# Two MLPs whose second product runs partly with seven block products: the order of the pairs in a job, the half of the features that is summed, and when weights are asked for

## The chip, the cores and the metric

One core of a Trainium2 chip runs the whole program. The metric is the time of the program on the device in microseconds (us), the median of several runs. Engines by the names of the profile: PE is TensorE (PEld its weight loads), DVE is VectorE, ACT is ScalarE, POOL is GpSimd, SP is SyncE. PSUM has eight banks here, which the kernel calls mm (four), sb (two) and tb (two).

## What is computed

A decoder trunk of two layers on 256 tokens of 2048 features in float32. Each layer has an attention part, which the change does not touch, and an MLP:

```python
def sq_relu_mlp(h, w1, w2):
    return jnp.square(jax.nn.relu(h @ w1)) @ w2      # w1 2048 x 8192, w2 8192 x 2048
...
f = sq_relu_mlp(rms_norm(h, g_ffn_pre), *ffns[layer])
h = h + rms_norm(f, g_ffn_post)
```

## The kernel before

Every float32 operand is cut in two (`split`: a rounded high part by ACT, L246 or with the norm's gain L249; the rest by DVE, L247 or L250), and a product is three matmuls: high by high, high by low, low by high.

An MLP runs over four blocks of 2048 of the 8192 features. In a block **ff1** makes the block's features from `uT` and `w1`, in two jobs of 1024 features (`job_T`): eight units of 128 features, each in a PSUM bank of its own, over 16 k of 128 rows, two k at a time; a k of a unit is a matmul of 512 columns (L409) and one of 256 (L413). (The first half of block 0 is done by other jobs.) When a unit is complete, ACT copies (L402) and DVE adds (L403) its halves; of two units ACT then does relu and square (L733, L734) and the split into `hT`: a pair of 128-feature tiles, eight pairs in a block. Pairs 0 to 3 come from ff1's first job, 4 to 7 from its second.

**ff2** multiplies the block by its rows of `w2`, in two jobs of 1024 output columns, c = 0 and c = 1 (`job_7`). Each job goes over the eight pairs. A *plain* pair is 2x2 blocks times 2x2 blocks with 8 products. A *seven* is the same with 7 products of sums of blocks, into eight banks c11, c12, c21, c22 (as in a plain pair) and p1, p5, p6, p7, which are put together later. A seven needs sums of features (`Sevens.put`: DVE L485 to L489, then a split, `sums`) and sums of weights (DVE L525 to L527, `wsum`, whose split is `wboth`). Each product is three matmuls of 512 columns (L564). The order is 0, 4, 1, 5, 2, 6, 3, 7, with 4 to 7 sevens. So a job has 4 x 8 + 4 x 7 = 60 products, 180 matmuls, and it ends on a seven. In block 3 only c = 0 is done so; c = 1 is a plain job.

In blocks 0 to 2 each of the eight banks that a job ends with is copied by ACT to one of six tiles `s` (L767) and added by a DMA of POOL into `acc` in DRAM, 256 KB each (plain writes in block 0, L769; accumulating ones from block 1 on, L771). In block 3 `combine` (L783) reads them all back by SP's queue while ff1's first job runs, and DVE adds them up (L796).

The c banks are mm; p1 and p6 are sb; p5 and p7 are tb. The units of an ff1 job take mm x4, sb x2, tb x2 (`all_banks`). Weights come by SP's queue into three 1 MB tiles `raw`; each job's own generator asks for a `raw` and its split just ahead of the matmuls that use them in the written order. A scheduler then sets the order of each engine; the time of a wait is read from the trace only.

## Time and profile before

| | us |
|---|---|
| median of 3 runs | 2341.24 (2337.76 to 2345.25) |
| the profiled execution | 2339.55 |
| its span, first to last instruction | 2337.8 |
| PE busy | 2256.1 (97%) |
| DVE, ACT, POOL busy | 1624.5, 1405.9, 128.7 |
| mean granted clock of PE | 0.983 |

The span is one execution; the 1.75 us between it and the execution's time lie around it. A busy share is an average over all stages, so a stage has to be read by itself: its length against the matmuls in it, and what PE waits for there. The granted clock is 1.00 at 2.4 GHz and 0.50 at 1.2 GHz.

### The profile page before, as it was taken

To read this page: it belongs to the slowest core of one execution; us is meant where nothing else is said; L and a number is where in the kernel's file an instruction comes from. 1 tells how busy PE (TensorE), PEld (TensorE's weight loads), DVE (VectorE), ACT (ScalarE), POOL (GpSimd) and SP (SyncE) were. 2 spreads that over 40 slices of the span, in tenths; PEclk is the share of its full clock that TensorE was granted. 3 is DMA by queue.
4 is the path that set the end of the run, shared out by engine and by line. 5 is a ranking of instruction groups with operands and counts; after the bars stand their busy time and mean duration, and the time that the engine had idled before them with its cause. 6 is when DMAs were issued, how large, how long until landed. Compare 5 with 4: busy or idle time off the path is not lost. (4 is left out here: it accounts for less than half of the span.)

```text
span 2337.8 us, 31006 instructions
## 1 busy us (share of the span) xinstructions
PE 2256.1 (97%) x11781; PEld 1921.1 (82%) x11781; DVE 1624.5 (69%) x2483; ACT 1405.9 (60%) x2180; POOL 128.7 (6%) x144
## 2 busy tenths in 40 slices
PE   9999999999999999999999999999999999989997
PEld 8889888788788877877888888887788877877876
DVE  5877557695685687597565677847695685587586
ACT  5766557565565665576556666657565665564664
POOL 0000010000011011001000000011000011011002
PEclk9999999999999999999999999999999999999999
DMA  7744346466477479554554554555476477559653
GB/s 243 240 145 149 132 164 216 159 237 232 158 241 232 162 214 293 198 221 179 192 194 148 182 167 159 178 180 198 144 249 239 160 233 219 196 167 294 223 204 138
DMA packets 148722, 460.60 MB, mean 197 GB/s; under 512 B 9046, under 2 KB 9820, under 8 KB 147036
## 3 DMA queue, kind: packets, MB, share of 16 engines
q1 hardware_dynamic: 136220, 429.25, 53.5%
q0 software_dynamic: 12352, 29.37, 5.7%
q8 instruction: 92, 1.51, 0.3%
q14 instruction: 58, 0.48, 0.1%
HBM read 427.12 MB, written 31.46 MB: 196 GB/s over the span
## 5 line engine op out<-in xcount | busy, mean ns | idle before, releaser
L250 DVE SCALAR_TENSOR_TENSOR wlo<-raw,gT,whi 128x512 fp32r<-128x512 f32 (+4 forms) x621 | 606.6, 1009 | 404.3 <-PE tb L413 168.5
L249 ACT ACTIVATE whi<-raw,gT 128x512 fp32r<-128x512 f32 (+4 forms) x621 | 551.4, 928 | 401.1 <-PE tb L409 187.7
L409 PE MATMUL mm<-uT,whi 128*128 128x512 f32 x1952 | 504.4, 394 | 1.2 <-ACT whi L249 0.9
L247 DVE TENSOR_TENSOR wlo<-raw,whi 128x1024 fp32r<-128x1024 f32 x304 | 374.3, 1245 | 139.1 <-ACT whi L246 134.2
L246 ACT ACTIVATE whi<-raw 128x1024 fp32r<-128x1024 f32 x304 | 313.2, 1055 | 147.7 <-PE mm L365 66.7
L409 PEld LDWEIGHTS mm<-uT,whi 128*128 128x128 f32 x1952 | 347.3, 189 | 59.9 <-ACT whi L249 1.4
L564 PE MATMUL mm<-whi,hT 128*128 128x512 f32 x1120 | 359.9, 393 | 0.0
L413 PEld LDWEIGHTS mm<-uT,wlo 128*128 128x128 f32 x1952 | 273.9, 192 | 25.0 <-DVE wlo L250 2.3
L413 PE MATMUL mm<-uT,wlo 128*128 128x256 f32 x1952 | 283.3, 284 | 2.0 <-DVE wlo L250 2.0
L564 PEld LDWEIGHTS mm<-whi,hT 128*128 128x128 f32 x1120 | 212.9, 190 | 44.7
L564 PE MATMUL mm<-wlo,hT 128*128 128x512 f32 x560 | 219.5, 392 | 0.6 <-DVE wlo L247 0.6
L365 PE MATMUL mm<-whi,uT 128*128 128x512 f32 (+1 forms) x640 | 197.0, 398 | 0.0
L564 PE MATMUL tb<-wboth,sums 128*128 128x512 f32 x336 | 100.9, 425 | 35.0 <-ACT wboth L246 35.0
L365 PEld LDWEIGHTS mm<-whi,uT 128*128 128x128 f32 x640 | 115.9, 189 | 19.7
L409 PE MATMUL tb<-uT,whi 128*128 128x512 f32 x448 | 125.3, 395 | 5.8 <-ACT s L767 5.8
L409 PE MATMUL sb<-uT,whi 128*128 128x512 f32 x448 | 123.5, 391 | 4.4 <-ACT s L767 4.4
L564 PEld LDWEIGHTS mm<-wlo,hT 128*128 128x128 f32 x560 | 105.6, 189 | 25.2 <-DVE wlo L247 3.6
L564 PEld LDWEIGHTS tb<-wboth,sums 128*128 128x128 f32 x336 | 66.9, 204 | 54.0 <-ACT wboth L246 38.4
L246 ACT ACTIVATE wboth<-wsum 128x1024 fp32r<-128x1024 f32 x56 | 59.5, 1062 | 85.8 <-DVE wsum L525 84.0
L365 PE MATMUL mm<-wlo,uT 128*128 128x512 f32 x320 | 104.8, 385 | 1.1 <-DVE wlo L250 1.1
L409 PEld LDWEIGHTS tb<-uT,whi 128*128 128x128 f32 x448 | 81.4, 189 | 23.6 <-ACT s L767 7.6
L409 PEld LDWEIGHTS sb<-uT,whi 128*128 128x128 f32 x448 | 81.8, 188 | 21.1 <-ACT s L767 6.1
(305 smaller groups left out, 3186.2 us busy)
## 6 DMA issues: line engine op xcount, KB each, us to landing
raw<-in_l_w_ff_dram SPq DMA_DIRECT2D x256, 1024.0 KB, 5.0
raw<-in_l_w_in_dram SPq DMA_DIRECT2D x87, 1024.0 KB, 5.1
raw<-in_l_w_out_dram SPq DMA_DIRECT2D x24, 1024.0 KB, 4.8
raw<-in_l_w_in_dram SPq DMA_DIRECT2D x8, 832.0 KB, 4.6
acc0c<-s POOLq DMA_DIRECT2D x24, 256.0 KB, 7.4
acc0p<-s POOLq DMA_DIRECT2D x24, 256.0 KB, 10.9
acc1c<-s POOLq DMA_DIRECT2D x24, 256.0 KB, 7.2
acc1p<-s POOLq DMA_DIRECT2D x24, 256.0 KB, 10.3
```

The costliest lines, as they stand in the source:

```text
L246: nc.scalar.activation(hi, src, AF.Copy)
L247: eng.tensor_tensor(lo, src, hi.bitcast(F), ALU.subtract)
L249: nc.scalar.activation(hi, src, AF.Copy, scale=scale)
L250: nc.vector.scalar_tensor_tensor(lo, src, scale, hi.bitcast(F), ALU.mult, ALU.subtract)
L365: nc.tensor.matmul(ps[t, c][:, 0:w], xs, ws[:, offs[c]:offs[c] + w], start=(k == 0 and p == 0), stop=(k == nk - 1 and p == 2))
L409: nc.tensor.matmul(ps[b], wt[0][:, fs], mov.both(k), start=(k == 0), stop=False, skip_group_check=True)
L413: nc.tensor.matmul(ps[b][:, 0:SEQ], wt[1][:, fs], mov.at(k)[0], start=False, stop=(k == nk - 1), skip_group_check=True)
L564: nc.tensor.matmul(ps[b], xs, ws, start=first and p == 0, stop=last[b] == (j, i) and p == 2, skip_group_check=True)
```

## The change

- **Order in a job of ff2.** A table gives each job's pairs and which are sevens. c = 0 goes 0, 4, 5 plain, 1 seven, 6 plain, 2, 3 seven, 7 plain: three sevens, so 61 products and 183 matmuls. c = 1 goes 4 plain, 0 seven, 5 plain, 1 seven, 6 plain, 2, 3 seven, 7 plain: still four sevens and 180 matmuls. Both end on a plain pair, whose products are sorted by bank, so that c11, c12, c21, c22 end one after the other, two products each.
- **Sums.** The sevens are among pairs 0 to 3, ff1's first half, so `sums` are made while ff1's second job runs. In block 0, where pairs 0 and 1 come out of another job, `put_parts` first adds their two parts again.
- **Weights.** Each job's generator is wrapped in a `Stream`, and `ahead` asks for a pair's `raw` and split one pair early, the next job's first ones included (two k of `w1`, one pair of `w2`).
- **Banks.** c11 and c12 are sb, c21 and c22 are tb, the four p are mm. ff1 takes sb x2, tb x2, mm x4.
- **What goes to DRAM.** The four p are copied into one 1 MB tile `side` and go out in one DMA when p7 is done; the four c as before. Five DMAs a job in place of eight; `combine` reads `side` back by one DMA in place of four. In block 3 DVE adds the c from PSUM, without ACT's copy.
- **keep.** The write of the residual `h` to DRAM in block 0 stands ahead of ff1's second half.

```diff
         wts = [next(gen) for _ in range(last)]
+        if ahead:
+            ahead()
...
+        def put_parts(self, pair):
+            v = self.stat.parts[pair // 2][:, pair % 2 * 2:pair % 2 * 2 + 2, :, :].bitcast(F)
+            y = s2()
+            nc.vector.tensor_tensor(
+                y.rearrange("p (k q) -> p k q", k=2), v[:, :, 0, :], v[:, :, 1, :], ALU.add)
+            self.put(pair, y)
...
-        for pair in order:
...
+        for pair, by7 in order:
...
-            if pair not in sevens.pairs:
+            if not by7:
...
-    LAST_SEVEN = tuple(SEVEN[i] for i in (0, 1, 6, 2, 4, 3, 5))
...
+        def ahead(self, n=1):
+            self.held.extend(next(self.gen) for _ in range(n))
...
+        def __next__(self):
+            return self.held.popleft() if self.held else next(self.gen)
...
-        def seq_of(pair):
-            if pair in sevens.pairs:
-                return LAST_SEVEN if pair == order[-1] else SEVEN
-            return tuple((f"c{t + 1}{n + 1}", (t, k), (k, n)) for k in range(2) for t in range(T) for n in range(2))
...
+        def seq_of(j):
+            pair, by7 = order[j]
+            if by7:
+                return SEVEN
+            kk = tuple((f"c{t + 1}{n + 1}", (t, k), (k, n)) for k in range(2) for t in range(T) for n in range(2))
+            return kk if j < len(order) - 1 else tuple(sorted(kk, key=lambda e: e[0]))
...
+        if not gen.held:
...
             parts = next(gen)
...
+            if j + 1 < len(order):
+                gen.ahead()
+            else:
+                ahead()
+            for i, (b, which, form) in enumerate(seqs[j]):
...
-                    ps[b] = (mm_bank if b[0] == "c" else s_bank if b in ("p1", "p6") else t_bank)()
+                    ps[b] = {"c1": s_bank, "c2": t_bank}.get(b[0:2], mm_bank)()
...
-        order = [p for i in range(nk // 4) for p in (i, nk // 4 + i)]
-        BANKS = ("c11", "c12", "c21", "c22", "p1", "p5", "p6", "p7")
...
+        ORDERS = (((0, 0), (4, 0), (5, 0), (1, 1), (6, 0), (2, 1), (3, 1), (7, 0)),
+                  ((4, 0), (0, 1), (5, 0), (1, 1), (6, 0), (2, 1), (3, 1), (7, 0)))
+        SIDE = ("p1", "p6", "p5", "p7")
...
+        side = [dram.tile([P, 4, 512], F, name=f"side{c}", tag=f"{gname}side{c}") for c in range(2)]
...
-            c0 = 0
             if b == 0:
                 job(uT, w1, 0, KT, [(0, 512)], evac, gT=gT, g0=g0, first=8)
-                job_T(uT, w1, 0, KT, (512, 512), evac_T(4), gT=gT, g0=g0, first=4, last=4,
-                      run=4)
-                c0 = 1024
-            for c in range(c0, FBLK, 1024):
-                job_T(uT, w1, 0, KT, (b * FBLK + c, 1024), evac_T(c // P), gT=gT, g0=g0, bank=all_banks(), first=2,
-                      last=2, run=2)
-        def ff2(b, sevens, c, evac):
-            job_7(sevens, w2, b * nk, c * 1024, order, evac)
+                for pair in range(2):
+                    later(sevens.put_parts, pair)
+                job_T(uT, w1, 0, KT, (512, 512), evac_T(4), gT=gT, g0=g0, first=4, last=4, run=4)
+                bt.flush()
+                for t in range(T):
+                    keep(t)
+            for i, gen in enumerate(gens):
...
+                job_T(uT, w1, 0, KT, (b * FBLK + c, 1024), evac_T(c // P), gT=gT, g0=g0, bank=all_banks(4), first=2,
+                      last=2, run=2, gen=gen, ahead=(lambda: then.ahead(2)) if then else nxt.ahead)
...
+            how = {} if b == 0 else dict(accum_op=ALU.add)
+            st = []
             def f(name, ps):
+                if name in SIDE:
+                    if not st:
+                        st.append(A([P, 4, 512], F, "side"))
+                    nc.scalar.activation(st[0][:, SIDE.index(name), :], ps, AF.Copy)
+                    if name == SIDE[-1]:
+                        nc.gpsimd.dma_start(side[c], st[0], **how)
+                    return
                 y = s2()
                 nc.scalar.activation(y, ps, AF.Copy)
-                if b == 0:
-                    nc.gpsimd.dma_start(acc[c][name], y)
-                else:
-                    nc.gpsimd.dma_start(acc[c][name], y, accum_op=ALU.add)
+                nc.gpsimd.dma_start(acc[c][int(name[1]) - 1, int(name[2]) - 1], y, **how)
...
-            for i, name in enumerate(BANKS[4:]):
-                p[name] = pt[:, i, :]
-                nc.sync.dma_start(p[name], acc[c][name])
+            nc.sync.dma_start(pt, side[c])
...
-                    nc.sync.dma_start(out_of(m, c, t, n), acc[c][f"c{t + 1}{n + 1}"])
+                    nc.sync.dma_start(out_of(m, c, t, n), acc[c][t, n])
...
-                got[name] = y = s2()
-                nc.scalar.activation(y, ps, AF.Copy)
...
+                if name in SIDE:
+                    got[name] = s2()
+                    nc.scalar.activation(got[name], ps, AF.Copy)
...
+                t, n = int(name[1]) - 1, int(name[2]) - 1
+                add(out_of(m, c, t, n), ps, out_of(m, c, t, n), ALU.add)
+                pn.chunk_done(t, 2 * c + n)
...
+        w1s = [w1_stream(0, 1024)]
...
-            sevens = Sevens(hT, tuple(range(nk // 4, nk // 2)))
+            sevens = Sevens(hT, tuple(range(nk // 4)))
...
+            w2s = [w2_stream(b, 0), None if end else w2_stream(b, 1)]
+            ff1(b, hT, sevens, w1s, w2s[0])
+            bt.flush()
...
-                for c in range(2):
-                    ff2(b, sevens, c, to_acc(b, c))
+                w1s = [w1_stream(b + 1, c) for c in range(0, FBLK, 1024)]
+                job_7(sevens, w2s[0], ORDERS[0], to_acc(b, 0), w2s[1].ahead)
+                job_7(sevens, w2s[1], ORDERS[1], to_acc(b, 1), lambda: w1s[0].ahead(2))
...
+            gen = Stream(weights(w2, b * nk, nk, chunks512(1024)))
+            job_7(sevens, w2s[0], ORDERS[0], into(pn, 0, m), lambda: gen.ahead(2))
...
+            job(hT, w2, b * nk, nk, chunks512(1024), evac, last=4, after=lambda t: pn.finish(t, then), gen=gen)
```

ACT where ff1 of block 1 ends and ff2 begins, first MLP. `hT` and `sums` are the pairs' splits; `whi` and `wboth` are high parts of `w2`. Before:

```order
L402 ACTIVATE s2_5915<-tb_5536 128x256
L402 ACTIVATE s2_5915<-tb_5537 128x256
L246 ACTIVATE sums_5149<-s2_5905 128x512
L733 ACTIVATE s2_5915<-s2_5915 128x512
L734 ACTIVATE s2_5915<-s2_5915 128x512
L246 ACTIVATE hT_5147<-s2_5915 128x2x256
L246 ACTIVATE wboth_5986<-wsum_5974 128x1024
L246 ACTIVATE whi_5982<-raw_5972 128x1024
L246 ACTIVATE sums_5149<-s2_5928 128x512
L246 ACTIVATE whi_5989<-wsum_5974 128x512
```

After (L403, L769, L770 are L402, L733, L734 of before; `whi_5928` belongs to pair 4, `whi_5962` and `whi_5966` to pair 5, `whi_6000` and `wboth_6008` to pair 1, the first seven):

```order
L769 ACTIVATE s2_5892<-s2_5892 128x512
L403 ACTIVATE s2_5909<-mm_5549 128x256
L770 ACTIVATE s2_5892<-s2_5892 128x512
L246 ACTIVATE whi_5928<-raw_5922 128x1024
L246 ACTIVATE hT_5135<-s2_5892 128x2x256
L769 ACTIVATE s2_5909<-s2_5909 128x512
L246 ACTIVATE whi_5962<-raw_5960 128x1024
L770 ACTIVATE s2_5909<-s2_5909 128x512
L246 ACTIVATE whi_5966<-raw_5960 128x1024
L246 ACTIVATE hT_5135<-s2_5909 128x2x256
L246 ACTIVATE whi_6000<-raw_5994 128x1024
L246 ACTIVATE wboth_6008<-wsum_5996 128x1024
```

The `sums` are gone from this place, and `whi` of plain pairs stand between the pairs' evacuations; the first `wboth` is still behind the last `hT`.

ACT where ff2 of block 1 ends and ff1 of block 2 begins: copies of banks (`s2`, `side`) and high parts of `w1` (L249). Before:

```order
L249 ACTIVATE whi_6626<-raw_6620,gT_945 128x1024
L767 ACTIVATE s2_6567<-mm_6280 128x512
L767 ACTIVATE s2_6573<-mm_6284 128x512
L767 ACTIVATE s2_6579<-mm_6288 128x512
L767 ACTIVATE s2_6585<-sb_6335 128x512
L767 ACTIVATE s2_6591<-tb_6343 128x512
L249 ACTIVATE whi_6664<-raw_6662,gT_945 128x1024
L767 ACTIVATE s2_6597<-sb_6339 128x512
L767 ACTIVATE s2_6603<-tb_6347 128x512
L249 ACTIVATE whi_6668<-raw_6662,gT_945 128x1024
```

After:

```order
L815 ACTIVATE side_6510<-mm_6317 128x512
L815 ACTIVATE side_6510<-mm_6321 128x512
L249 ACTIVATE whi_6622<-raw_6620,gT_945 128x1024
L820 ACTIVATE s2_6544<-sb_6265 128x512
L820 ACTIVATE s2_6553<-sb_6269 128x512
L820 ACTIVATE s2_6562<-tb_6273 128x512
L249 ACTIVATE whi_6626<-raw_6620,gT_945 128x1024
L820 ACTIVATE s2_6571<-tb_6277 128x512
```

The copies of p stand before those of the c banks, and the last copy is that of c22, with `whi` of the next job ahead of it.

PE where ff1's first job of block 1 hands over to its second (xN stands for N matmuls). The first rows end the first job's last units; the rest is the second job. Before:

```order
L409 MATMUL tb<-uT,whi 128x512 x2
L413 MATMUL tb<-uT,wlo 128x256 x2
L409 MATMUL tb<-uT,whi 128x512 x2
L413 MATMUL tb<-uT,wlo 128x256 x2
L409 MATMUL mm<-uT,whi 128x512 x8
L409 MATMUL sb<-uT,whi 128x512 x4
L409 MATMUL tb<-uT,whi 128x512 x4
L413 MATMUL mm<-uT,wlo 128x256 x8
```

After:

```order
L410 MATMUL mm<-uT,whi 128x512 x2
L414 MATMUL mm<-uT,wlo 128x256 x2
L410 MATMUL sb<-uT,whi 128x512 x4
L410 MATMUL tb<-uT,whi 128x512 x4
L414 MATMUL sb<-uT,wlo 128x256 x4
L414 MATMUL tb<-uT,wlo 128x256 x4
L410 MATMUL sb<-uT,whi 128x512 x4
L410 MATMUL tb<-uT,whi 128x512 x4
L414 MATMUL sb<-uT,wlo 128x256 x4
L414 MATMUL tb<-uT,wlo 128x256 x4
L410 MATMUL sb<-uT,whi 128x512 x2
L410 MATMUL mm<-uT,whi 128x512 x2
```

Before, the second job begins on four mm banks. Now it begins on sb and tb, does four k there, and comes to the first mm bank after 32 matmuls and two of the next k.

## Rows read from the trace of the kernel before

**Rows 1.** Part 1 of the page: busy us (share of the span), instructions.

```profile
PE 2256.1 (97%) x11781; PEld 1921.1 (82%) x11781; DVE 1624.5 (69%) x2483; ACT 1405.9 (60%) x2180; POOL 128.7 (6%) x144
```

**Rows 2.** Windows, ff2's first job: the first of eight, and their sum.

```profile
core 0: us, PE busy (x) PEld busy (x) DVE busy (x) ACT busy (x) POOL busy (x), PEclk, DMA share, GB/s
444.90:493.70 48.80, 43.90 (x181) 35.15 (x181) 45.75 (x63) 34.36 (x48) 2.69 (x5) 0.93 0.48 164
...
sum 391.20, PE 351.17 PEld 281.37 DVE 366.39 ACT 275.64 POOL 17.90; mean PE 43.90 PEld 35.17 DVE 45.80 ACT 34.45 POOL 2.24
```

**Rows 3.** Windows, ff2's second job: two of six, and sum.

```profile
493.70:534.50 40.80, 40.80 (x181) 33.78 (x180) 32.72 (x33) 26.40 (x33) 4.27 (x8) 1.00 0.74 258
671.90:715.10 43.20, 42.07 (x182) 33.39 (x180) 32.53 (x33) 26.28 (x33) 6.97 (x10) 1.00 0.79 238
...
sum 253.20, PE 248.84 PEld 201.62 DVE 198.82 ACT 157.90 POOL 35.65; mean PE 41.47 PEld 33.60 DVE 33.14 ACT 26.32 POOL 5.94
```

**Rows 4.** Windows, ff1's first job: one of six, and sum.

```profile
534.50:579.00 44.50, 44.50 (x257) 39.27 (x256) 22.98 (x22) 22.89 (x28) 1.62 (x4) 1.00 0.70 246
...
sum 289.00, PE 275.85 PEld 240.33 DVE 154.18 ACT 137.35 POOL 20.11; mean PE 45.97 PEld 40.05 DVE 25.70 ACT 22.89 POOL 3.35
```

**Rows 5.** Windows, ff1's second job: the sum of six.

```profile
sum 267.40, PE 267.40 PEld 234.94 DVE 151.24 ACT 151.85 POOL 0.00; mean PE 44.57 PEld 39.16 DVE 25.21 ACT 25.31 POOL 0.00
```

**Rows 6.** TensorE's timeline, end of ff1 in block 1: start, length, [idle before <-releaser].

```profile
630.18 0.39 PE L564 MATMUL mm<-whi,sums 128*128 128x512 f32 x1
634.95 1.22 PE L564 MATMUL tb<-wboth,sums 128*128 128x512 f32 x2 [4.38 <-ACT wboth L246]
636.69 0.79 PE L564 MATMUL sb<-whi,hT 128*128 128x512 f32 x1 [0.52 <-ACT whi L246]
```

**Rows 7.** ScalarE's timeline, the same place.

```profile
624.14 0.63 ACT L246 ACTIVATE sums<-s 128x512 fp32r<-128x512 f32 x1 [0.41 <-DVE s L489]
...
627.73 0.63 ACT L246 ACTIVATE sums<-s 128x512 fp32r<-128x512 f32 x1 [0.41 <-DVE s L489]
...
633.85 1.05 ACT L246 ACTIVATE wboth<-wsum 128x1024 fp32r<-128x1024 f32 x1
```

**Rows 8.** Waits: us in total, times, longest; the wait of rows 6.

```profile
PE tb L564 <- ACT wboth L246: 35.0, 8, 4.4
```

**Rows 9.** Narrow windows around three waits; columns as in rows 2.

```profile
634.90:639.90 5.00, 4.43 (x10) 2.88 (x11) 5.00 (x9) 4.32 (x6) 0.00 (x0) 0.50 0.01 3
...
721.90:725.20 3.30, 3.30 (x15) 3.09 (x15) 2.48 (x2) 3.30 (x4) 0.83 (x1) 0.50 1.14 216
...
680.10:687.00 6.90, 6.90 (x30) 5.71 (x31) 6.90 (x8) 5.09 (x6) 0.00 (x0) 1.00 1.10 260
```

**Rows 10.** TensorE's timeline, from ff2 to ff1 (block 1 to block 2).

```profile
721.63 1.05 PE L409 MATMUL tb<-uT,whi 128*128 128x512 f32 x2 [2.23 <-ACT s L767]
```

**Rows 11.** ScalarE's timeline, the same place.

```profile
720.98 0.60 ACT L767 ACTIVATE s<-tb 128x512 f32<-128x512 f32 x1 [2.82 <-DMA acc1c<-s]
```

**Rows 12.** TensorE's timeline, early in ff2's second job of block 1.

```profile
680.07 0.50 PE L564 MATMUL sb<-wlo,hT 128*128 128x512 f32 x1 [0.77 <-DVE wlo L247]
```

**Rows 13.** TensorE's timeline, block 3's combine.

```profile
2161.71 1.40 PE L413 MATMUL mm<-uT,wlo 128*128 128x256 f32 x7 [1.96 <-DVE wlo L250]
```

**Rows 14.** ScalarE's timeline, the same place.

```profile
2162.08 2.19 ACT L249 ACTIVATE whi<-raw,gT 128x1024 fp32r<-128x1024 f32 x2 [9.58 <-DMA raw<-in_l_w_ff_dram]
```

**Rows 15.** Parts 3 and 6 of the page: a queue; issues, KB each, us to landing.

```profile
q0 software_dynamic: 12352, 29.37, 5.7%
...
acc0p<-s POOLq DMA_DIRECT2D x24, 256.0 KB, 10.9
```

**Rows 16.** DMA issues of the whole run; a plain write of 1 MB.

```profile
kept<-h POOLq DMA_DIRECT2D x4, 1024.0 KB, 5.0
```

114 lines of the change are left out of this document (55 added, 59 removed).

## The prediction

> **What bounds the kernel now.** The page's first part comes first: PE is busy 2256 of 2338 us, and no other engine above 69% [rows 1]. So a gain comes from time in which PE waits, from time that it spends at a low clock, or from fewer matmuls. The second view is windows cut at the ends of the MLPs' jobs, whose length is set against their matmuls. An ff2 second job that nothing disturbs takes 40.80 us for 180 matmuls at granted clock 1.00 [rows 3]: 40.80 / 180 = 0.2267 us a matmul. First jobs of ff2 have the same 180 matmuls and take 48.9 us in the mean of eight (391.2 / 8) at a clock of 0.93 [rows 2]. Undisturbed first jobs of ff1 take 44.50, the six together 289.0 instead of 267.0 [rows 4]; the six second jobs are full, 267.4 [rows 5]. So the jobs lose: ff2 first, 391.2 - 8 x 40.8 = 64.8; ff2 second, 253.2 - 6 x 40.8 = 8.4; ff1 first, 22.0. That is 95 us, all in the neighbourhood of hand-overs.
>
> The third view is the timelines at those places. **ff1 to ff2** (eight places): PE does pair 0 and the first products of pair 4, then waits 4.38 us for `wboth` and 0.52 for `whi` [rows 6], eight times, 35.0 us in all [rows 8]. ACT is the one that is late: it has the relu, square, `hT` split and `sums` of four pairs to do, one pair in 3.59 us (624.14 to 627.73), 0.41 of it waiting for DVE, and `wboth` stands behind the last [rows 7]. After the wait PE runs at 0.50, that is 1.2 GHz [rows 9], and the window's loss of half its work is the rest of the 8.1 us a place (48.9 - 40.8). **ff2 to ff1** (four of six places; after block 0's plain writes it is clean): PE waits 2.23 us for the copy of a tb bank [rows 10], and that copy waited 2.82 us for an `s` tile whose accumulating DMA was under way [rows 11]; here too a stretch at 0.50 follows [rows 9]. **Early in ff2's second job**, waits such as 0.77 us for a `wlo` [rows 12], with the clock at 1.00 afterwards [rows 9]. **Block 3's combine**: 1.96 us of PE [rows 13], where ACT got its `raw` 9.58 us late [rows 14], behind the reads of `acc` in SP's queue.
>
> **The change part by part.**
>
> *The added product.* Each of eight first jobs of ff2 has 61 products for 60: 3 x 0.2267 = 0.68 us, 5.4 in all. PE is what sets the end there, so it counts in full.
>
> *ff1 to ff2.* Four `sums` splits (0.63 each, with a 0.41 wait) leave ACT's path, so a pair takes about 2.6 instead of 3.59 us, and three plain pairs stand first, 72 matmuls or 16.3 us of PE for which no sum is needed. Let E be ff1's end. ACT begins on the first pair some 4.7 us before E (a pair of units is 1.4 us of PE, three pairs of units and a copy), needs 4 x 2.6 = 10.4, and then, by its order, six `whi` or `wboth` of 1.05 [rows 7] and a small one: 7.0. The first seven is complete at E + 12.7, and PE wants it at E + 16.3: 3.6 us to spare. Pair 5, wanted at E + 10.9, has its two `whi` ahead of the last `hT`, at about E + 9. So I cost the wait at nothing, and the cover is PE's three plain pairs. The job then takes 40.8 + 0.68 = 41.5, and eight of them 332.0 for 391.2: **-59.2**.
>
> *Early in the second job.* The first pair's weights are asked for a pair earlier, 5.4 us, against waits below 2.4 us a job (43.2 - 40.8) [rows 3]; its banks c are sb and tb, free as the first job's last copies are done, 1 us after its end, while c22 is first wanted 2 us in. 6 x 40.8 = 244.8: **-8.4**.
>
> *ff2 to ff1.* The last pair ends its banks 1.36 us apart (six matmuls), and the p are copied well before. ACT's copies of c21 and c22 (0.6 each [rows 11]) with a `whi` between them end about 1.05 us after the job; PE wants c22's bank with the fourth unit, 6 x 0.2267 = 1.36 us in. Four `s` tiles a job of six no longer run round within one burst, so a copy meets a tile filled 40 us earlier. 6 x 44.5 = 267.0 for 289.0: **-22.0**. The clock's loss goes with the waits.
>
> *First to second job of ff1.* This is where work is put that was not there. The four `sums` (0.63 of ACT each) now stand between evacuations, and the pair whose mm banks come last must be free for the second job. Before, PE went on without loss there [rows 5]. Now it does sb and tb first: 32 matmuls and two more, 6.0 us, then the first mm unit, and the last two mm units at 9.7 us. By ACT's order with two `whi` a pair those banks are free at 5.6 to 6.1 and 9.2 to 10.4 us. So the wait is between 0 and 0.9 us for the later one, and I take 0.9 at six places since the sums of times there leave no slack: **+5.4**. Bounds: nothing, and one pair's 3.59 us [rows 7] with half of a 3.30 us stretch at 0.50 [rows 9], 5.2 a place.
>
> *Block 3's combine.* One read of `side` and four of `acc` take SP's queue in place of eight, at the same place, and the bytes are the same. PE's wait of 1.96 us with its clock was in ff1's first job, and I have already taken that job at 44.5. Bounds a place: nothing, or the old 1.96 with half of 3.30; I take the middle, 2.0 at two places: **+4.0**.
>
> *DMA out.* One accumulating DMA of 1 MB replaces four of 256 KB. No row shows one; a plain 1 MB write lands in 5.0 us [rows 16], an accumulating 256 KB in 10.9 [rows 15]. I cost it at nothing: by its place it is issued before the job's end, and no buffer of its own is wanted again within 30 us. *keep*, block 0's extra additions and DVE's adds from PSUM in block 3 lie beside full PE: DVE is busy 69% [rows 1] and its share falls by the removed copies; nothing.
>
> **Sum.** -59.2 - 8.4 - 22.0 + 5.4 + 4.0 = -80.2. From the profiled execution, 2339.55, that gives 2259.35. The median of the runs stands 1.7 above it, so **2261.0**. With both unknown terms at nothing it is 2251.6, and a run's spread of 3 us is below that: 2249.
>
> **The rivals.**
>
> *The combine still holds the weights up.* For: ACT's `raw` came 9.58 us late [rows 14], and the wait chain is SP's, which the change only shortens. With the full delay on PE's path less what a pair ahead covers, some 11 us a place: 2 x 11 - 4 = +18, 2279. Against: before, the same delay cost PE 1.96. Chance 0.11.
>
> *ff1's second job waits for its mm banks.* The sums moved into ACT's busiest place. At the upper bound, 6 x 5.2 - 5.4 = +26: 2287. Against: ACT is idle for 19 of 44.6 us there (25.31 busy in the mean [rows 5]). Chance 0.07.
>
> *The clock falls at short waits.* If each wait below 1 us that the sum leaves (six hand-overs, two places in block 3) drew a stretch at 0.50 as after the 2.23 us wait [rows 9, 10], that is 8 x 1.65 = +13: 2274. Against: after the 0.77 us wait the clock was 1.00 [rows 9, 12]. Chance 0.08. The Trainium skill has a rule on this side ("TensorE: Matmul & The Clock Gate", section "A second HAM failure mode: psum-queue depth-cycling"): short idles of PE between groups of matmuls, as it goes from bank to bank, make the clock swing. By that rule it is 2274 and not 2261; the row of 680.1 us speaks against it.
>
> *The change does not do all that it says.* ACT's order puts `whi` between evacuations; were the first seven 4 us later than worked out, half of the old 8.1 us a place stayed: 8 x 4.05 = +32, 2293. Against: the 3.6 us to spare. Chance 0.05. If nothing were gained on the whole, another 0.01, within 0.3%.
>
> *Slower: the 1 MB accumulating DMA.* If its time goes by its bytes, 4 x 10.9 = 43.6 us after issue [rows 15]. The thirteen large tiles go round, and `side`'s is wanted again for a `wboth` of the next job some 30 us later, so PE would stand 13.6 us in six second jobs, 82. In block 3 the read of `side` is due some 17 us after the last issue, and the weights queued behind it on SP would wait 26.6 at two places, 53. Together +135: 2396. It decides from a landing later than 30 us. Against: four of 256 KB are under way at once now and all land in some 11 us, and the queue's share is 5.7% [rows 15]. Chance 0.02.
>
> **How the numbers follow.** The forecast, 2249 to 2268, gets 0.66; the combine 0.11, short waits 0.08, ff1's banks 0.07, half a gain 0.05, no gain 0.01, the slow DMA 0.02. The range 2249 to 2284 holds the first three cases and part of the fourth. A measurement of this kernel tells about 0.3% (7 us) from no change, so: faster 0.97, same 0.01, slower 0.02.
>
> **What would show it.** First jobs of ff2 at 41.5 us with clock 1.00 and no wait of PE for `wboth`; second jobs at 40.8; first jobs of ff1 at 44.5, with no wait for a copy; second jobs of ff1 above 44.6 by no more than 1 us. PE's busy time should fall too, to about 2225 us, since matmuls at 1.2 GHz go. The forecast is wrong if a stretch at 0.50 stays anywhere between the jobs, if `side` lands more than 30 us after its issue, or if PE waits for an mm bank in ff1's second job.

## The result, and the profile after

The changed kernel takes 2275.35 us (median of 4 runs, 2270.78 to 2276.11) against 2341.34 for the kernel before, measured beside it: a ratio of 0.9714, 95% interval 0.9694 to 0.9734. The forecast was 2261.0, in a range of 2249 to 2284. So the sign and most of the size came as worked out, and 14 us of the forecast gain did not come. The time lies in the range, but above the 2249 to 2268 of the forecast's own case; that part of the range was held by two rivals. The profiled execution took 2275.03 us, 15.7 above the 2259.35 of the sum.

The page of the changed kernel: busy time (part 1), POOL's DMA queue (part 3), and the landings of POOL's writes to `side` and `acc` (part 6: count, KB each, median us). A third of these, those of block 0, are plain writes; the others accumulate.

```profile
PE 2236.6 (98%) x11805; PEld 1913.7 (84%) x11805; DVE 1588.2 (70%) x2447; ACT 1384.5 (61%) x2156; POOL 113.0 (5%) x108
...
q0 software_dynamic: 8192, 29.36, 5.3%
...
side<-side POOLq DMA_DIRECT2D x12, 1024.0 KB, 11.1
acc<-s POOLq DMA_DIRECT2D x48, 256.0 KB, 12.8
```

PE's busy time fell by 20 us, from 2256.1 [rows 1] to 2236.6; about 2225 was forecast. Its mean granted clock rose from 0.983 to 0.995, so its stretches at 1.2 GHz became fewer. A 256 KB write to `acc` now lands in 12.8 us at the median of all 48, where 10.9 was the slowest of four kinds [rows 15].

The same windows as before, cut at the ends of the jobs (us, busy time and instructions of each engine, PEclk, DMA share, GB/s). ff2's first jobs (one of eight and the sum), then its second jobs (one of six and the sum):

```profile
444.50:486.00 41.50, 41.50 (x186) 34.34 (x185) 38.33 (x42) 30.85 (x43) 1.90 (x4) 1.00 0.57 205
...
sum 332.00, PE 332.00 PEld 274.82 DVE 307.78 ACT 243.41 POOL 19.13; mean PE 41.50 PEld 34.35 DVE 38.47 ACT 30.43 POOL 2.39
...
831.00:875.60 44.60, 42.78 (x182) 34.88 (x182) 31.74 (x32) 25.73 (x32) 4.38 (x6) 0.96 0.79 241
...
sum 252.10, PE 248.84 PEld 203.11 DVE 190.62 ACT 154.73 POOL 22.44; mean PE 41.47 PEld 33.85 DVE 31.77 ACT 25.79 POOL 3.74
```

ff1's first jobs (three of six and the sum), then its second jobs (one and the sum):

```profile
526.80:571.30 44.50, 44.50 (x257) 39.25 (x256) 21.49 (x21) 20.62 (x24) 0.79 (x2) 1.00 0.67 241
...
875.60:925.60 50.00, 46.85 (x258) 40.35 (x257) 31.48 (x37) 20.59 (x24) 1.44 (x2) 0.97 0.91 296
...
2077.50:2129.70 52.20, 47.54 (x258) 40.51 (x257) 31.07 (x36) 20.36 (x23) 1.48 (x2) 0.97 0.88 286
sum 280.30, PE 272.49 PEld 237.94 DVE 149.12 ACT 123.63 POOL 7.79; mean PE 45.41 PEld 39.66 DVE 24.85 ACT 20.61 POOL 1.30
...
571.30:616.60 45.30, 45.12 (x259) 39.14 (x257) 30.72 (x45) 29.61 (x43) 0.00 (x0) 1.00 0.54 187
...
sum 272.00, PE 270.60 PEld 234.65 DVE 184.45 ACT 177.85 POOL 0.00; mean PE 45.10 PEld 39.11 DVE 30.74 ACT 29.64 POOL 0.00
```

Against the working, job by job, in us:

| | before | forecast | after |
|---|---|---|---|
| ff2, first jobs (8) [rows 2] | 391.2 | 332.0 | 332.0 |
| ff2, second jobs (6) [rows 3] | 253.2 | 244.8 | 252.1 |
| ff1, first jobs (6) [rows 4] | 289.0 | 267.0, and 4.0 for the combine | 280.3 |
| ff1, second jobs (6) [rows 5] | 267.4 | 272.8 | 272.0 |

The first and the last line came as worked out. The miss is +7.3 in the second line and +9.3 in the third, less 0.8: 15.8, which is the whole of it. In the third line four jobs are at 44.5 or 44.6 and block 3's two at 50.0 and 52.2.

Where ff2's second jobs lose. Block 2 of the first MLP loses most, 44.6 us for 40.8. First the timelines of DVE and PE (start, length, [idle before <-releaser]):

```profile
840.31 1.23 DVE L540 TENSOR_TENSOR wsum<-raw 128x1024 f32<-128x1024 f32 x1 [6.78 <-DMA raw<-in_l_w_ff_dram]
...
843.45 0.50 PE L595 MATMUL sb<-wlo,hT 128*128 128x512 f32 x1 [1.82 <-DVE wlo L247]
```

Then the DMA issues of two windows of 5 us, 827 to 832 and 832 to 837 (count, KB each, us to landing):

```profile
side<-side POOLq DMA_DIRECT2D x1, 1024.0 KB, 11.2
raw<-in_l_w_ff_dram SPq DMA_DIRECT2D x1, 1024.0 KB, 13.1
acc<-s POOLq DMA_DIRECT2D x3, 256.0 KB, 13.7
...
raw<-in_l_w_ff_dram SPq DMA_DIRECT2D x1, 1024.0 KB, 12.3
```

A weight tile that lands in 5.0 us at the median of the whole run takes 13.1 and 12.3 us while the side tile and the four c are being accumulated. DVE stands 6.78 us until it has landed, PE waits 1.82 us, and a stretch at a lower clock follows (PEclk 0.96 in the window of 831.00).

Three other second jobs lose 0.8 to 1.7 us each. There the longest wait of DVE's `wsum` ends with the side tile's DMA. Block 1 of the first MLP, timeline of DVE:

```profile
665.35 1.23 DVE L540 TENSOR_TENSOR wsum<-raw 128x1024 f32<-128x1024 f32 x1 [4.75 <-DMA side<-side]
```

POOL issued that DMA at 653.77, 11.6 us earlier. The large tiles are handed out in turn, and `wsum` needs the one that the DMA still reads.

Where block 3 loses. The timelines of SP's queue, of ACT and of PE:

```profile
871.81 0.39 SPq L314 DMA_DIRECT2D raw<-in_l_w_ff_dram  x1
882.77 0.32 SPq L846 DMA_DIRECT2D pt<-side  x1
884.76 8.22 SPq L849 DMA_DIRECT2D m<-acc  x4
893.07 12.17 SPq L314 DMA_DIRECT2D raw<-in_l_w_ff_dram  x4
...
893.41 2.19 ACT L249 ACTIVATE whi<-raw,gT 128x1024 fp32r<-128x1024 f32 x2 [13.07 <-DMA raw<-in_l_w_ff_dram]
...
894.61 0.50 PE L410 MATMUL sb<-uT,whi 128*128 128x512 f32 x1 [2.12 <-ACT whi L249]
```

The second combine's five reads (882.77 and 884.76) stand in SP's queue until their accumulating DMAs, issued up to 877, have landed; from 872.2 to 893.07 no weight is asked for. By the waits of SP's queue, 10.5 us of this is for `side`'s DMA and 8.3 us for those of `acc`. ACT waits 13.07 us for its `raw`, where it waited 9.58 before [rows 14], and PE waits 2.12 us and more.

### The profile page after: what moved, and what is told of

It is laid out like the page before. It is cut to its first block, busy times and chain, and to the rows that moved or that the text cites. A ratio compares the mean times of both kernels' runs of the same rounds, so it can differ in the third digit from the quotient of the medians.

```text
span 2273.0 us, 30826 instructions
## 1 busy us (share of the span) xinstructions
PE 2236.6 (98%) x11805; PEld 1913.7 (84%) x11805; DVE 1588.2 (70%) x2447; ACT 1384.5 (61%) x2156; POOL 113.0 (5%) x108
## 3 DMA queue, kind: packets, MB, share of 16 engines
q0 software_dynamic: 8192, 29.36, 5.3%
## 4 chain that ended last, share of the span: by engine, by line
PE 33%; issue 18%; DVE 3%; POOL 2%; DMA 2%; ACT 1%; SPq 0%; DVEq 0%; POOLq 0%; ACTq 0%
PE mm L410 10%; PE mm L365 8%; PE mm L414 5%; PE sb L595 2%; PE tb L595 2%; PE tb L410 1%; PE sb L410 1%; POOL m L721 1%; DMA m<-acc 1%; PE mm L595 1%; DVE wlo L247 1%; PE sb L671 1%; PE tb L414 1%; PE sb L414 1%; DVE h L735 1%
## 5 line engine op out<-in xcount | busy, mean ns | idle before, releaser
L249 ACT ACTIVATE whi<-raw,gT 128x512 fp32r<-128x512 f32 (+4 forms) x621 | 553.2, 927 | 380.7 <-PE mm L410 227.1
L410 PEld LDWEIGHTS mm<-uT,whi 128*128 128x128 f32 x1952 | 352.0, 189 | 66.2 <-issue 3.9
L414 PEld LDWEIGHTS mm<-uT,wlo 128*128 128x128 f32 x1952 | 268.2, 191 | 17.0
L595 PE MATMUL tb<-whi,hT 128*128 128x512 f32 x608 | 214.3, 390 | 0.0
L595 PE MATMUL sb<-whi,hT 128*128 128x512 f32 x608 | 214.1, 390 | 0.0
L595 PEld LDWEIGHTS tb<-whi,hT 128*128 128x128 f32 x608 | 114.7, 189 | 24.0
L595 PEld LDWEIGHTS sb<-whi,hT 128*128 128x128 f32 x608 | 114.4, 188 | 23.3
L595 PE MATMUL sb<-wlo,hT 128*128 128x512 f32 x304 | 119.7, 394 | 3.3 <-DVE wlo L247 3.3
L595 PE MATMUL tb<-wlo,hT 128*128 128x512 f32 x304 | 118.8, 391 | 0.0
L410 PEld LDWEIGHTS sb<-uT,whi 128*128 128x128 f32 x448 | 76.2, 191 | 16.6 <-ACT whi L249 8.2
L246 ACT ACTIVATE wboth<-wsum 128x1024 fp32r<-128x1024 f32 x48 | 50.9, 1061 | 61.7 <-DVE wsum L540 61.7
## 6 DMA issues: line engine op xcount, KB each, us to landing
side<-side POOLq DMA_DIRECT2D x12, 1024.0 KB, 11.1
acc<-s POOLq DMA_DIRECT2D x48, 256.0 KB, 12.8
```

Source lines behind the costliest of these rows:

```text
L246: nc.scalar.activation(hi, src, AF.Copy)
L249: nc.scalar.activation(hi, src, AF.Copy, scale=scale)
L410: nc.tensor.matmul(ps[b], wt[0][:, fs], mov.both(k), start=(k == 0), stop=False, skip_group_check=True)
L414: nc.tensor.matmul(ps[b][:, 0:SEQ], wt[1][:, fs], mov.at(k)[0], start=False, stop=(k == nk - 1), skip_group_check=True)
L595: nc.tensor.matmul(ps[b], xs, ws, start=first and p == 0, stop=last[b] == (j, i) and p == 2, skip_group_check=True)
```

## The experiments

The theory: the gain comes from PE work that needs nothing new (plain pairs) in front of each ff2 job, and from copies of banks that no longer wait for tiles; what is missing is the work of the accumulating DMAs. The rivals: the requests a pair ahead, the new place of the sums, the plain pair at the end, the places of the banks. Sums of windows below are of the same stages as above. The median of the kernel before, measured beside each set of runs, lay between 2337.90 and 2341.34 us, so a difference of 3 us between two sets shows nothing by itself; the sums of windows tell more.

### e1: without the requests ahead

```diff
         def ahead(self, n=1):
-            self.held.extend(next(self.gen) for _ in range(n))
+            pass
...
-            return self.held.popleft() if self.held else next(self.gen)
+            return next(self.gen)
```

> The changed kernel with its requests a pair ahead taken away: each pair's weights are asked for just before its own matmuls in the written order, everything else as changed. Theory (the order of the pairs and the place of the sums took the 35 us wait for wboth away; asking ahead only helps at the seams): ff2's first jobs stay near 41.5 to 43 us each, no wait of PE for wboth of 4 us, and the time is 5 to 25 us above the changed kernel's 2275, say 2280 to 2300. Rival (asking ahead is what removed it): the 4.4 us wait and the stretch at clock 0.50 come back at eight places, ff2's first jobs at 47 to 49 us, 2320 to 2340.

Measured 2272.51 us (2271.75 to 2276.02), ratio 0.9714 (0.9699 to 0.9728): no slower than with them, and below what theory and rival expected. ff2's first jobs sum to 332.0 as with them. Its second jobs:

```profile
sum 250.00, PE 247.77 PEld 201.99 DVE 190.60 ACT 154.67 POOL 22.06; mean PE 41.29 PEld 33.66 DVE 31.77 ACT 25.78 POOL 3.68
```

250.0 against 252.1. The edit moved hardly any request: SP's queue issues the weights of block 1's ff2 from 623.04 us with the requests ahead and from 623.17 without. What the queue waits for from 616 to 700 us is the same line in both kernels (us in total, times, longest):

```profile
SPq L524 <- DVE wlo L247: 63.7, 12, 10.9
```

A weight tile is asked for when DVE's `wlo` has freed one of the three, whatever the written order says. So asking a pair ahead in the written order is worth nothing that can be measured here, and the step of the prediction that gave it 8.4 us falls.

### e2: sums from the second half again

```diff
-        ORDERS = (((0, 0), (4, 0), (5, 0), (1, 1), (6, 0), (2, 1), (3, 1), (7, 0)),
-                  ((4, 0), (0, 1), (5, 0), (1, 1), (6, 0), (2, 1), (3, 1), (7, 0)))
+        ORDERS = (((0, 0), (1, 0), (2, 0), (4, 1), (7, 0), (5, 1), (6, 1), (3, 0)),
+                  ((0, 0), (4, 1), (1, 0), (5, 1), (2, 0), (6, 1), (7, 1), (3, 0)))
...
-                for pair in range(2):
-                    later(sevens.put_parts, pair)
...
-            sevens = Sevens(hT, tuple(range(nk // 4)))
+            sevens = Sevens(hT, tuple(range(nk // 4, nk // 2)))
```

> The changed kernel with the sevens taken from the second half of the features again (pairs 4 to 7), with plain pairs 0, 1, 2 first and 3 last in ff2's first job: the sums splits stand again between the evacuations at ff1's end and are gone from the seam inside ff1. Theory (three plain pairs ahead of the first seven, 16.3 us, are the cover; ACT then needs about 4.1 us more and ends at about 16.7 us): a wait of 0 to 1 us at eight places, and the 0.9 us at six seams inside ff1 is gone, so 2270 to 2282. Rival (it is the place of the sums that counts): waits of 2 to 4 us with a stretch at clock 0.50 come back at eight places, 2300 to 2340.

Measured 2275.06 us (2274.41 to 2276.33): the same time. ff2's first jobs, then ff1's second jobs:

```profile
sum 333.60, PE 333.60 PEld 274.20 DVE 322.12 ACT 256.59 POOL 14.44; mean PE 41.70 PEld 34.27 DVE 40.26 ACT 32.07 POOL 1.80
...
sum 267.40, PE 267.40 PEld 234.89 DVE 151.36 ACT 151.86 POOL 0.00; mean PE 44.57 PEld 39.15 DVE 25.23 ACT 25.31 POOL 0.00
```

The first jobs lose 0.2 us each (333.6 for 332.0), no more, so with three plain pairs in front the new place of the sums is not needed to remove the wait for `wboth`. ff1's second jobs are full again, 267.4: the 0.8 us a seam is the sums. What is won there, 4.6, is lost again, 1.6 here and 2.5 in ff2's second jobs (254.6 for 252.1).

### e3: a seven at the end

```diff
-        ORDERS = (((0, 0), (4, 0), (5, 0), (1, 1), (6, 0), (2, 1), (3, 1), (7, 0)),
-                  ((4, 0), (0, 1), (5, 0), (1, 1), (6, 0), (2, 1), (3, 1), (7, 0)))
+        ORDERS = (((0, 0), (4, 0), (5, 0), (1, 1), (6, 0), (2, 1), (7, 0), (3, 1)),
+                  ((4, 0), (0, 1), (5, 0), (1, 1), (6, 0), (2, 1), (7, 0), (3, 1)))
```

> The changed kernel with the last two pairs of each ff2 job exchanged: it ends on a seven (pair 3) and not on a plain pair. Theory (the wait from ff2 to ff1 was the s tiles' wait for DMAs, and it is gone since four copies go to a side tile and only four to s tiles): the seam stays without a wait of more than 0.5 us, within 5 us of 2275. Rival (the plain pair at the end is what frees the banks in time): 2 to 3 us and a stretch at 0.50 at six places come back, ff1's first jobs at 48 to 50 us, 2295 to 2305.

Measured 2277.91 us (2275.47 to 2279.63), 2.6 above the change and within the theory's 5. ff1's first jobs sum to 282.2 for 280.3; the four of blocks 1 and 2 lose 0.1 us each in the mean (44.6 to 44.7), the rest is in block 3. So the plain pair at the end is worth next to nothing at the seam.

### e4: plain writes

```diff
-            how = {} if b == 0 else dict(accum_op=ALU.add)
+            how = {}
```

> The changed kernel with plain writes in place of all accumulating DMAs (so the sums over blocks 0 to 2 are left out: only the last block's part is kept). Theory (what is left of the loss comes from the accumulating DMAs: while they are under way a 1 MB raw lands in 12 to 13 us and not 5, and block 3's reads wait for them in SP's queue): ff2's second jobs all at 40.8 us (4 of 6 lose 0.8 to 3.7 us now), block 3's first ff1 jobs at 44.5 to 47 (50.0 and 52.2 now), 2257 to 2267. Rival (the amount of reading and the order on SP's queue make the loss whatever the kind of write): within 4 us of 2275.

This kernel leaves out the sums over the blocks. Measured 2255.30 us (2254.30 to 2256.01), ratio 0.9637 (0.9622 to 0.9651), a little below the theory's span. ff2's second jobs, then ff1's first jobs:

```profile
sum 244.80, PE 244.80 PEld 202.70 DVE 191.74 ACT 156.67 POOL 16.18; mean PE 40.80 PEld 33.78 DVE 31.96 ACT 26.11 POOL 2.70
...
sum 267.50, PE 267.30 PEld 235.48 DVE 148.65 ACT 122.83 POOL 4.80; mean PE 44.55 PEld 39.25 DVE 24.77 ACT 20.47 POOL 0.80
```

POOL's queue and the landings of its DMAs:

```profile
q0 software_dynamic: 6144, 29.36, 3.5%
...
side<-side POOLq DMA_DIRECT2D x12, 1024.0 KB, 7.1
acc<-s POOLq DMA_DIRECT2D x48, 256.0 KB, 7.0
```

With the same bytes and the same reads, written plainly, the second jobs are at 40.8 each and block 3 loses 0.5 us. The 256 KB land in 7.0 us for 12.8, the 1 MB in 7.1 for 11.1. The two losses of the change, 7.3 and 13.3, are 20.6, and 20 us go. So the cause is that the DMAs accumulate, not the amount that is read back. The run does not part the ways in which they cost: their tiles come free sooner, two weight tiles asked for beside them (824 to 834 us) land in 8.9 us at the median where 13.1 and 12.3 stood, and SP's queue asks for no weight for 12.6 us (867.2 to 879.8) in place of 20.9.

### e5: the kernel before, with plain pairs in front

```diff
-        order = [p for i in range(nk // 4) for p in (i, nk // 4 + i)]
+        order = [0, 1, 2, 4, 3, 5, 6, 7]
```

> The kernel before with one edit: the pairs of both ff2 jobs go 0, 1, 2, 4, 3, 5, 6, 7, so that three plain pairs stand ahead of the first seven; sevens, sums, banks, DMAs and requests as before, no product added. Theory (three plain pairs in front are what covers ACT at ff1's end): the wait for wboth and the stretch at 0.50 go at eight places, ff2's first jobs at 40.8 to 42 for 48.9, the seams from ff2 to ff1 stay as they were: 2340 - 55 to 65 = 2275 to 2285, as fast as the whole change. Rival (plain pairs in front alone are not enough, sums or requests have to move as well): half the wait stays, 2300 to 2320.

Measured 2293.11 us (2290.57 to 2293.72), ratio 0.9798 (0.9783 to 0.9813): one line gives 46 of the change's 66 us. First and second jobs of ff2, first jobs of ff1:

```profile
sum 334.00, PE 333.62 PEld 267.43 DVE 330.47 ACT 248.31 POOL 13.69; mean PE 41.70 PEld 33.43 DVE 41.31 ACT 31.04 POOL 1.71
...
sum 267.40, PE 251.81 PEld 200.84 DVE 225.58 ACT 173.52 POOL 40.03; mean PE 41.97 PEld 33.47 DVE 37.60 ACT 28.92 POOL 6.67
...
sum 282.40, PE 271.82 PEld 237.64 DVE 151.39 ACT 134.22 POOL 19.70; mean PE 45.30 PEld 39.61 DVE 25.23 ACT 22.37 POOL 3.28
```

The wait at ff1's end is gone (334.0 for 391.2; 326.4 would be none), with sums, banks and requests as they were. The theory's place is right, and the time is above its 2275 to 2285 for a reason that neither side had: ff2's second jobs got worse, 267.4 for 253.2. PE waits there for `wlo`, 1.73 us the longest in block 1, and ACT for a `raw`, 3.2 us the longest. At the seam to ff1, where nothing was edited, blocks 1 and 2 show no loss (44.5 to 44.7 each). In block 3's two (52.1 each) the old wait stands: a copy waits 4.9 and 4.8 us for an `s` tile, and PE 2.7 us behind it. That PE only comes later to the seams of blocks 1 and 2, after its loss in the second job, is a guess that was not tested.

### e6: the second combine later

```diff
         def combine(m, c):
+            for _ in range(8 * c):
+                yield
             pt = A([P, 4, 512], F, "pt")
```

> The changed kernel with the reads of block 3's second combine asked for eight steps of some 1.3 us later, about 10 us. Theory (SP's queue is held by these reads, which wait for the accumulating DMAs to land some 15 us after ff1's start, so weights behind them come late): the loss in block 3's first ff1 jobs, 5.6 and 7.8 us now, falls to 0 to 2 each, 2262 to 2268. Rival (the DMA engines are full in that time, whatever stands in SP's queue): the loss stays at 4 us or more each, 2270 to 2276.

Measured 2269.88 us (2268.57 to 2271.62), 5.5 below the change. ff1's first jobs:

```profile
sum 275.60, PE 269.94 PEld 236.67 DVE 148.13 ACT 123.47 POOL 8.35; mean PE 44.99 PEld 39.45 DVE 24.69 ACT 20.58 POOL 1.39
```

275.6 for 280.3: about a third of block 3's 13 us loss. The number falls between the theory's 2262 to 2268 and the rival's 2270 to 2276: the place of the reads in SP's queue is one part, and full DMA engines (share 0.91 and 0.88 in the change's two windows) may be the other. The share alone does not make the loss: in e9, below, these windows have 0.97 and lose 2.3 and 1.7 us.

### e7: the banks as before

```diff
-                    ps[b] = {"c1": s_bank, "c2": t_bank}.get(b[0:2], mm_bank)()
+                    ps[b] = (mm_bank if b[0] == "c" else s_bank if b in ("p1", "p6") else t_bank)()
...
-bank=all_banks(4)
+bank=all_banks()
```

> The changed kernel with the banks as before: c on mm, p1 and p6 on sb, p5 and p7 on tb, and ff1's units beginning on mm. Theory (the 0.9 us at six seams inside ff1 comes from the second job's last mm units, whose banks are evacuated last; with mm first they are free early, and the plain end still frees c11 to c22 in time): ff1's second jobs at 44.5, 2270, that is 5 us less. Rival (the new places of c and p are needed for the seam from ff2 to ff1 or from ff1 to ff2): a new wait at one of these, 2280 or more.

Measured 2273.25 us (2271.09 to 2277.57): the same. Both expectations fall. The seam inside ff1 of block 1 in the changed kernel, timelines of PE and DVE:

```profile
581.67 1.17 PE L410 MATMUL mm<-uT,whi 128*128 128x512 f32 x4 [0.18 <-DVE s L404]
...
581.11 0.75 DVE L404 TENSOR_TENSOR s<-mm,s 128x256 f32<-128x256 f32 x2
```

PE at the same place with the old banks:

```profile
581.43 1.17 PE L410 MATMUL tb<-uT,whi 128*128 128x512 f32 x4 [0.18 <-DVE s L404]
```

PE waits at the same moment for the same thing, the last two units' banks: mm there, tb here. What is late is the last pair's evacuation behind the sums (without sums there, in e2, the loss is gone), and the bank's name has no part in it.

### e8: a fourth raw tile

```diff
-    NA, NW = 13, 5
+    NA, NW = 12, 5
...
-    wraw = ctx.enter_context(tc.tile_pool(name="wraw", bufs=3))
+    wraw = ctx.enter_context(tc.tile_pool(name="wraw", bufs=4))
```

> The changed kernel with four raw tiles of weights for three (and twelve of the large tiles for thirteen). Theory (accumulating DMAs make a 1 MB raw land in 13 us for 5, and three raw tiles reach only some 10 us ahead): a fourth reaches one pair further, the loss of ff2's second jobs (7 us in four of them) falls under 2, block 3's under half, 2258 to 2270. Rival (the loss comes from the sevens' other tiles or from one tile less): within 4 us of 2275 or above.

Measured 2264.27 us (2263.38 to 2265.10), ratio 0.9677 (0.9662 to 0.9691), 11 below the change. ff2's second jobs, ff1's first jobs:

```profile
sum 244.80, PE 244.80 PEld 202.72 DVE 199.73 ACT 160.40 POOL 22.66; mean PE 40.80 PEld 33.79 DVE 33.29 ACT 26.73 POOL 3.78
...
sum 276.90, PE 272.03 PEld 237.88 DVE 148.31 ACT 123.06 POOL 7.35; mean PE 45.34 PEld 39.65 DVE 24.72 ACT 20.51 POOL 1.23
```

The second jobs are at 40.8 each, with the accumulating DMAs in place: one more megabyte under way covers the late landings. The edit also takes one large tile away, and the two halves were not run apart; DVE's waits for the side tile are gone, and ACT waits for it instead, 14.1 us in four places, at no cost to these jobs. Block 3 keeps 9.9 us of its 13.3, more than the half expected.

### e9: the fourth raw tile and the later combine

Both edits together.

> The changed kernel with four raw tiles (and twelve large ones) and with the second combine's reads asked for eight steps later. Theory (two separate faults: raw tiles reach too short a way ahead while accumulating DMAs run, and the combine's reads hold SP's queue): what the fourth tile left in block 3, 4.8 and 5.3 us, falls to 0 to 2 each, 2256 to 2261. Rival (both help against the same lateness): no more than 2 us below the 2264 of the fourth tile alone.

Measured 2258.48 us (2258.18 to 2259.25), ratio 0.9658 (0.9643 to 0.9672), 17 below the change and the fastest of the kernels with the whole computation. ff1's first jobs:

```profile
871.80:918.60 46.80, 45.12 (x258) 39.30 (x257) 31.05 (x37) 20.64 (x24) 1.44 (x2) 1.00 0.97 318
...
sum 271.30, PE 268.26 PEld 235.74 DVE 148.18 ACT 123.36 POOL 7.50; mean PE 44.71 PEld 39.29 DVE 24.70 ACT 20.56 POOL 1.25
```

271.3, where 271.0 was forecast for the change itself. The two edits help against two faults: 5.8 us from the second, on top of the first.

### e10: four sevens in ff2's first job

On e9, the first job in the order of the second.

```diff
-        ORDERS = (((0, 0), (4, 0), (5, 0), (1, 1), (6, 0), (2, 1), (3, 1), (7, 0)),
-                  ((4, 0), (0, 1), (5, 0), (1, 1), (6, 0), (2, 1), (3, 1), (7, 0)))
+        ORDERS = (((4, 0), (0, 1), (5, 0), (1, 1), (6, 0), (2, 1), (3, 1), (7, 0)),) * 2
```

> As the kernel with four raw tiles and the later reads, and ff2's first job in the order of its second: pair 4 plain first, pair 0 a seven, four sevens, so 180 matmuls and no plain pair from the first half in front. Theory (the cover at ff1's end is PE work that needs nothing of ff1's last units; pair 0 in front is part of it): eight jobs gain 0.68 us each and lose more, a wait of 1 to 3 us at ff1's end with a stretch at 0.50 in some, 8 to 30 us slower than that kernel. Rival (two plain pairs around one seven are cover enough): up to 5 us faster than it.

Measured 2269.83 us (2268.33 to 2270.07), 11 above e9. First jobs and second jobs:

```profile
sum 329.90, PE 329.71 PEld 270.46 DVE 323.15 ACT 244.66 POOL 14.96; mean PE 41.21 PEld 33.81 DVE 40.39 ACT 30.58 POOL 1.87
...
sum 254.40, PE 249.27 PEld 201.90 DVE 203.19 ACT 157.78 POOL 23.20; mean PE 41.54 PEld 33.65 DVE 33.87 ACT 26.30 POOL 3.87
```

A wait of the whole run (us in total, times, longest):

```profile
ACT wboth L246 <- DMA side<-side: 33.2, 6, 7.2
```

The time is in the theory's span, but not by its mechanism. At ff1's end next to nothing is lost (329.9 for 326.4, 0.45 us a job, no stretch at 0.50); there the rival is right: with the sums made early, one plain pair in front is nearly enough. The loss is in the second jobs, 254.4 for 244.8: the twelve large tiles are handed out in turn, and with one seven more in the first job ACT waits 33.2 us in six waits for the tile that the side tile's DMA still reads (14.0 in four in e9). PE waits behind it; block 1's second job, timeline of PE:

```profile
669.08 1.43 PE L595 MATMUL mm<-wboth,sums 128*128 128x512 f32 x5 [0.76 <-DVE wboth L247]
```

A kernel with this order and thirteen large tiles was not run.

### e11: late sums on e9

The edit of e2 on e9.

> As the kernel with four raw tiles and the later reads, with sevens from the second half of the features (pairs 4 to 7; 0, 1, 2 plain in front, 3 plain at the end). Theory (the 0.9 us inside ff1 at six seams is the sums between evacuations and nothing else; at ff1's end three plain pairs cover them): six times 0.73 us gained and eight times 0.2 lost, 1 to 4 us faster than that kernel. Rival (sums at ff1's end cost again once weights come in time): 5 us or more slower.

Measured 2270.66 us (2270.24 to 2276.16), 12 above e9. The profiled execution is the slowest, 2276.16, so its sums overstate the loss by some 5 us. ff2's second jobs:

```profile
sum 258.80, PE 251.19 PEld 204.25 DVE 204.05 ACT 158.38 POOL 23.71; mean PE 41.87 PEld 34.04 DVE 34.01 ACT 26.40 POOL 3.95
```

The seam is full again, as expected (267.5), and more than that is lost in the second jobs (258.8 for 244.8), where ACT's `wboth` waits for the side tile's DMA as in e10, 36.3 us in six waits. ff2's first jobs lose 0.5 us each (335.9 for 332.0) where 0.2 was expected. So the rival's number came, but most of it by that wait, which neither side had named. In e2, the same order with thirteen large tiles, no `wboth` waits for the side tile.

### e12: without the side tile

```diff
                 if name in SIDE:
-                    if not st:
-                        st.append(A([P, 4, 512], F, "side"))
-                    nc.scalar.activation(st[0][:, SIDE.index(name), :], ps, AF.Copy)
-                    if name == SIDE[-1]:
-                        nc.gpsimd.dma_start(side[c], st[0], **how)
+                    nc.gpsimd.dma_start(side[c][:, SIDE.index(name), :], y, **how)
                     return
```

Here the copy into a tile `s` stands ahead of the branch, for c and p alike.

> The changed kernel with the side tile taken away: each p is copied to a tile s and goes out in its own 256 KB accumulating DMA, eight to a job as before; order, sums, banks and requests as changed. Theory (the wait from ff2 to ff1 came from six s tiles for eight copies, since the DMA of a tile takes 7 to 14 us): copies of c21 and c22 wait for a tile again, PE loses 2 to 5 us at four of six seams, and there are such waits between the two ff2 jobs, 2285 to 2305. Rival (the p are copied early enough by the plain pair at the end, or the tiles never were the limit): within 5 us of 2275.

Measured 2280.76 us (2279.57 to 2282.94), 5.4 above the change. ff1's first jobs (one of six, and the sum):

```profile
701.10:750.40 49.30, 46.41 (x258) 40.31 (x257) 21.53 (x21) 21.59 (x25) 1.72 (x2) 0.97 0.76 234
...
sum 286.90, PE 275.08 PEld 239.81 DVE 143.44 ACT 127.38 POOL 10.83; mean PE 45.85 PEld 39.97 DVE 23.91 ACT 21.23 POOL 1.81
```

Timelines of PE and ACT at the seam from block 1 to block 2:

```profile
705.57 1.22 PE L410 MATMUL tb<-uT,whi 128*128 128x512 f32 x2 [2.89 <-ACT s L813]
...
704.92 0.60 ACT L813 ACTIVATE s<-tb 128x512 f32<-128x512 f32 x1 [1.99 <-DMA side<-s]
```

The wait of rows 10 and 11 is back, 2.89 us of PE behind a copy that waited 1.99 us for a tile whose DMA was under way, with a stretch at a lower clock (PEclk 0.97), in spite of the plain pair at the end. So in this order of pairs the side tile is what ended it. The loss is smaller than expected: two seams of 5 to 6 us (49.3 and 50.2 for 44.5) and not four. Block 3's jobs are shorter here (47.2 and 49.4 for 50.0 and 52.2), and PE does not wait for a copy in them.

## Why the prediction was right, and where it was not

**ff1 to ff2: right.** The wait went, the stretch at 0.50 with it, and eight jobs take 332.0, as worked out, the added product included. That three plain pairs in front are cover enough is shown by e5 (on the kernel before, alone) and by e2 (sums back at ff1's end cost 0.2 us a job). They are not the only way: in e10, with the sums made early, one plain pair ahead of the first seven leaves only 0.45 us a job. So the plain pairs do it alone, and early sums, with the rest of the change around them, nearly do it without; the prediction, with both in one sum, did not part them. Its sum of times on ACT holds: in block 1 ACT ends the high parts of the first seven 12.4 us after ff1's end (628.97 - 616.60), where 12.7 was worked out, and PE comes to it at 632.95, 16.35 us after, where 16.3 was. It left DVE out, whose last low part for this seven is ready at 631.1, 1.8 us ahead of PE.

**ff2 to ff1: right in blocks 1 and 2, half right in cause.** Their four jobs came to 44.5 or 44.6. Block 3's two took 50.0 and 50.1 us before and 50.0 and 52.2 after, so of the 22.0 us only 8.7 came (289.0 - 280.3); the rest is the combine's, below. The prediction named the sorted end, the early copies of p and the tiles `s` together. e3 and e12 part them: the end is worth some 0.1 us a seam, while without the side tile the wait is back.

**First to second job of ff1: right.** 45.3 us for 44.5 at the seams, 4.6 in all where 5.4 was taken. PE waits for the last two mm units' evacuation and gets to them 10.4 us into the job (571.30 to 581.67); by the working they were wanted at 9.7 and free at 9.2 to 10.4. Without sums there (e2, e11) the loss is gone. The prediction named a wait for an mm bank here as a sign of being wrong, though its own sum had taken one in. The later idea that the banks' places matter (e7) was wrong, and is not in the prediction.

**Early in ff2's second job: the step that failed.** The prediction took the whole 8.4 us as gained, by asking a pair ahead. 1.1 came. The row it rested on, a `wlo` late by 0.77 us [rows 12], was read as a request that came late. The kernel before shows another cause at that very place, timelines of ACT and DVE:

```profile
677.22 0.60 ACT L767 ACTIVATE s<-tb 128x512 f32<-128x512 f32 x1 [4.23 <-DMA acc0c<-s]
...
678.79 1.23 DVE L247 TENSOR_TENSOR wlo<-raw,whi 128x1024 fp32r<-128x1024 f32 x1 [5.76 <-ACT whi L246]
```

ACT's copy of a tb bank waited 4.23 us for an `s` tile whose DMA was under way, and `whi`, then DVE's `wlo`, stood behind that copy: the fault of rows 11 once more. All four second jobs that lost time have such a wait, of 3.9 to 4.7 us. In the changed kernel no copy waits for an `s` tile there, so this loss went. The 7.3 us that are lost now are a new loss: a weight tile that lands late in block 2 and the side tile's DMA in three others. e1 shows that the requests ahead do nothing, e4 that the loss is the accumulating DMAs', e8 that one raw tile more (and one large tile less) covers it.

**Block 3's combine: a mis-sized term.** 4.0 was taken and 13.3 measured (280.3 - 267.0), in the rival's direction and short of its 22. The bound of the old wait was a place's price before; but the accumulating DMAs, of which the last is issued when the job ends, land later than before (12.8 us at the median; 10.9 was the slowest kind [rows 15]), and the five reads that wait for them hold SP's queue for 21 us. e6 shows that the place of these reads is part of the loss, not all of it. "The same place and the same bytes" left out what the reads wait for.

**DMA out: costed at nothing, wrong.** The side tile's DMA lands in 11.1 us, not in 43.6, so the slower rival did not come. But the 30 us until its tile is wanted again was wrong too: DVE's `wsum` waited for it in three places, 13.7 us in all:

```profile
DVE wsum L540 <- DMA side<-side: 13.7, 3, 4.8
```

These are the three second jobs that lose 0.8 to 1.7 us, so a part of the 7.3 may belong to this term. In e8 ACT waits for that tile at no cost; in e10 and e11 the wait reaches PE.

**Clock.** Short waits of PE at six seams inside ff1, 0.18 us in the row shown and 1.1 us in all six, left the clock at 1.00 (the window of 571.30), so the rival of the short waits did not come, although its 2274 is nearest to the measured time. After the wait of 1.82 us the clock fell (PEclk 0.96). The prediction named a stretch at 0.50 between the jobs as a sign of being wrong; those that stay stand in block 2's second job and in block 3 (PEclk 0.96 and 0.97), where the two terms above failed. The rule of the Trainium skill that the prediction weighed ("TensorE: Matmul & The Clock Gate", section "A second HAM failure mode: psum-queue depth-cycling") does not show at these seams.

Left open: why ff2's second jobs got worse in e5. Three sevens stand in a row at the end of its first job, and an order with the sevens apart was not run. Open too is what the rest of block 3's loss is, beside the place of the reads, and which half of e8's edit covers the second jobs.
